# A hybrid decoder trunk on one core: low parts of the mLSTM's queries and keys, a copy of the attention keys' low half, and the sum of sink and maximum, from VectorE to GpSimd

## The chip, the core and the metric

The kernel runs on one core of a Trainium2 chip. The engines of a core are TensorE (PE: matrix products and transposes into PSUM; PEld is its weight load), VectorE (DVE), ScalarE (ACT), GpSimd (POOL) and SyncE (SP, here a DMA queue). Each has an instruction stream of its own and works through it in order; an instruction that needs another engine's result waits on a semaphore, and whatever stands behind it on its engine waits too. The metric is the device time of one execution in microseconds (us), the median over runs.

## The reference, cut to what matters

Two layers on 512 tokens of width 1024, all in float32. Each layer normalises x, multiplies by one combined matrix W_in, runs two branches and merges them through sigmoid gates, then a squared-ReLU MLP follows.

```python
q_a, k_a, v_a, q_m, k_m, v_m, o_m, if_m, gates = jnp.split(h @ w_in, splits, axis=-1)
# branch A: causal attention, window 128, 8 query heads on 2 key heads, head dimension 64,
# queries and keys normalised and partly rotated, a learned sink per head
m = jnp.maximum(jnp.max(scores, axis=-1, keepdims=True), sink)
p = jnp.exp(scores - m)
probs = p / (jnp.sum(p, axis=-1, keepdims=True) + jnp.exp(sink - m))
out = probs @ v
# branch B: mLSTM (matrix memory, 4 heads, queries and keys of 64, values of 128)
w = jnp.exp(log_d - m_t) * (q @ k.T)
num, den = w @ v + ..., jnp.sum(w, -1) + ...
h = num / jnp.maximum(jnp.abs(den), jnp.exp(-m_t))
# merge
mixed = sigmoid(g_a) * (att @ w_att_branch) + sigmoid(g_m) * (hm @ w_m_branch)
x = x + mixed @ w_out
x = x + relu(rmsnorm(x) @ w_ff1) ** 2 @ w_ff2
```

## The kernel before, in words

**Precision by splitting.** Nearly every operand of a product is split into a high part (its copy in the type fp32r, on ACT) and a low part (the float32 value less the high part, on DVE), and a product is made of three matmuls: high by high, high by low, low by high (`mm3`, L214). For a weight tile of 128x512, `chunk` (L169) issues the load on SP's queue, the copy on ACT (L195) and the subtraction on DVE (L196).

**The main stream.** A layer's projections are chains of such products, in steps of 128 rows of the weights (`group_steps`, L219). `weave` (L257) goes through the steps with a running position, each step having a width (0.25 for one output tile of a group), and calls side work when the position reaches the place that the side work was given. Attention and the mLSTM are such side work. The stretch that concerns us is L761 to L869: the projections for the mLSTM's queries and keys, gates and values are the main stream; beside them run, for each block b of 128 tokens and each key head kv (8 units a layer):

- `rope` (L569) for queries and keys, on GpSimd but for the first multiplication;
- `q_tr` (L608): four transposes into one PSUM tile, then for two tiles and two halves of the partitions ACT copies the high part (L622) and DVE forms the low part (L623);
- `k_tr` (L591): a transpose of the keys; for each key head ACT writes the high part twice, into both halves of the partitions (L600, L601), DVE forms the low part in one half (L602) and copies it into the other (L603);
- `att_scores` (L626), twice for a unit: score matmuls into PSUM; the destination is filled with a large negative number by GpSimd for block 0 (L643) or filled by ACT (L645), and DVE copies where the mask allows (L646), which also frees the PSUM tile;
- `att_softmax` (L648): DVE reduces the maximum (L653) and forms m, the negated maximum of scores and sink (L654), and es = sink + m (L656); ACT takes four exponentials with their sums (L659) and the exponential of es (L661); DVE adds, inverts and multiplies (L662 to L664);
- `att_probs` (L666): transposes, a split (L207, L208), and for b > 0 four selects on GpSimd (L678, L680);
- `att_out` (L684): the product with the values, and its evacuation by ACT (L692) and DVE (L696), then a split into the branch's input (L699, L700).

`qk_split` (L716), eight times a layer, lays out the mLSTM's queries and keys for a product with the 64 channels in both halves of the partitions. For a query head the high part (ACT, L720) is copied by GpSimd into the other half (L722), and the low tile is cleared in one half by GpSimd (L724) and holds the subtraction in the other (DVE, L725). For a key head the high part is in one half and the subtraction goes straight into the other (DVE, L728). `m_weights` (L790) reads them after attention's stretch. `gating0` to `gating3` and the gates' evacuation (L746) are further side work on DVE.

PSUM for all this side work is two tiles that take turns (`aux`, L91). Small SBUF tiles come from rings: 24 slots of 128x512 (`slot`), 18 (`temp`).

**What sets the order.** The kernel is written against a tile framework. A planner in it goes through the program when it is built, with time estimates of its own: whenever an engine is free in its plan, the instruction comes next that is ready and stands earliest in the program (those under `tc.high_priority()` ahead of others). The instruction streams that result are fixed; on the chip each engine works its stream in order. The weight splits of `chunk` are under high priority. So an instruction that changes its engine or its duration in the plan can change the order on every engine. For example, L724 stands behind L722 in the code, but in the trace two L724 run on GpSimd from 66.13 us and the first L722 at 69.66 us.

Of the kernel before, what the change touches and what calls it, by code (L numbers as in the profile page):

```python
# [13 lines left out]
ALU = mybir.AluOpType  # L14
# [21 lines left out]
def hybrid_kernel(ctx, tc, x, norm_mix, w_in, att_q_norm, att_k_norm, att_sinks, m_gate_bias,  # L36
# [3 lines left out]
    ve, sc, gp = nc.vector, nc.scalar, nc.gpsimd  # L40
# [32 lines left out]
    def slot(dt=F32, shape=(P, T)):  # L73
        return now["act"].tile(list(shape), dt, tag="a", name=nm("a"))
# [16 lines left out]
    def aux(shape=(P, T)):  # L91
        return paux.tile(list(shape), F32, tag="aux", name=nm("aux"))

    def sm(shape, tag, bufs=None):
        return small.tile(list(shape), F32, tag=tag, name=nm(tag), bufs=bufs)

    def f32(ap):
        return ap.bitcast(F32)
# [40 lines left out]
    sinks = const.tile([P, DEPTH, HQ], F32, name="sinks")  # L139
# [294 lines left out]
    def mixer(l, norm, late, order, phase):  # L434
# [113 lines left out]
        for b in range(NB):  # L548
# [5 lines left out]
                         op=ALU.mult)  # L554
# [7 lines left out]
        kTh, kTl = kT[:, 0], kT[:, 1]  # L562
# [28 lines left out]
        def k_tr(b):  # L591

            ps = aux([P, P])
            pe.transpose(ps, kvi[:, b, 0:128], ident)
            for h in range(HKV):
                r = slice(64 * h, 64 * h + 64)
                o = slice(64 - 64 * h, 128 - 64 * h)
                c = slice((b + 1) * P, (b + 2) * P)
                g = gcols[1][r, l:l + 1]
                sc.activation(kTh[r, h, c], ps[r, :], AF.Copy, scale=g)  # L600
                sc.activation(kTh[o, h, c], ps[r, :], AF.Copy, scale=g)  # L601
                ve.scalar_tensor_tensor(kTl[r, h, c], ps[r, :], g, f32(kTh[r, h, c]), op0=ALU.mult, op1=ALU.subtract)  # L602
                ve.tensor_copy(kTl[o, h, c], f32(kTl[r, h, c]))  # L603

        def q_vec(b):
            rope(q_tok[b].rearrange("p (h d) -> p h d", d=HD), b, HQ)
# [41 lines left out]
        def att_softmax(b, kv):  # L648
            sp = sps[b, kv]
            s3 = sp.rearrange("p (h k) -> p h k", h=4)  # L650
            hs = slice(4 * kv, 4 * kv + 4)
            m = sm([P, 4], "m")
            ve.tensor_reduce(m, s3, axis=AX.X, op=ALU.max)  # L653
            ve.scalar_tensor_tensor(m, m, -1.0, nsinks[:, l, hs], op0=ALU.mult, op1=ALU.min)  # L654
            es = sm([P, 4], "es")
            ve.tensor_tensor(es, sinks[:, l, hs], m, op=ALU.add)  # L656
            den = sm([P, 4], "den")
            for i in range(4):
                sc.activation(s3[:, i, :], s3[:, i, :], AF.Exp, bias=m[:, i:i + 1],  # L659
                              accum_out=den[:, i:i + 1])  # L660
            sc.activation(es, es, AF.Exp)  # L661
            ve.tensor_tensor(den, den, es, op=ALU.add)  # L662
            ve.reciprocal(den, den)
            ve.tensor_tensor(s3, s3, den.unsqueeze(2).to_broadcast([P, 4, P]), op=ALU.mult)  # L664
# [51 lines left out]
        def qk_split(m, i):  # L716
            t = qk_raw[m]
            r, o = slice(64 * i, 64 * i + 64), slice(64 - 64 * i, 128 - 64 * i)
            d = slot(F32R)
            sc.activation(d[r], t[r], AF.Copy)  # L720
            if m < 2:
                gp.tensor_copy(d[o], f32(d[r]))  # L722
                low = slot(F32R)
                gp.memset(f32(low[o]), 0.0)  # L724
                ve.tensor_tensor(low[r], t[r], f32(d[r]), op=ALU.subtract)  # L725
                m_q[2 * m + i], m_ql[2 * m + i] = d, low
            else:
                ve.tensor_tensor(d[o], t[r], f32(d[r]), op=ALU.subtract)  # L728
                m_k[2 * (m - 2) + i] = d

        def sigmoid(tiles):
# [22 lines left out]
        def ev_v(b, ps):  # L754
            if b == 0:
# [5 lines left out]
        units = [(b, kv) for b in range(NB) for kv in range(HKV)]  # L761
        side = [(0, lambda: k_vec(0)), (0, lambda: q_vec(0)), (0, lambda: k_vec(1)), (0, lambda: q_vec(1)),
                (7 - 1.25, lambda: k_tr(0)), (7 - 1.75, lambda: q_tr(0))]
        for i, (b, kv) in enumerate(units):
            at = 7 + 1.65 * i
            side += [(at, lambda b=b, kv=kv: att_scores(b, kv, 0)),
                     (at + 1.25, lambda b=b, kv=kv: att_scores(b, kv, 1)),
                     (at + 1.25, lambda b=b, kv=kv: att_softmax(b, kv)),
                     (at + 3.45, lambda b=b, kv=kv: att_probs(b, kv)),
                     (at + 3.45 + 2.2, lambda b=b, kv=kv: att_out(b, kv))]  # L770
            if kv == 0 and b + 1 < NB:
                if b + 2 < NB:
                    side += [(at + 1, lambda b=b: k_vec(b + 2)), (at + 1, lambda b=b: q_vec(b + 2))]
                side += [(at + 2 * 1.65 - 1.25, lambda b=b: k_tr(b + 1)), (at + 2 * 1.65 - 1.75, lambda b=b: q_tr(b + 1))]
        side += [(8.45 + 3.0 * i, f) for i, f in enumerate((gating0, gating1, gating2, gating3))]
        side += [(9.6 + 1.65 * n, lambda n=n: qk_split(n // 2, n % 2)) for n in range(8)]
        g0, s0 = gate_steps(0)
        g1, s1 = gate_steps(1, lambda: back(sigmoid(g0 + g1)))
# [539 lines left out]
```

## Time and profile before

| | |
|---|---|
| median of 3 runs | 1310.29 us (1309.8 to 1310.82) |
| the profiled execution | 1310.1 us, of which the span from the first to the last instruction is 1308.4 us |
| granted TensorE clock | 1.000 |
| busy in the span | PE 1290.5 us, DVE 966.4 us, ACT 781.4 us, POOL 234.6 us |

The trace has one record for each instruction: its engine, line, start and duration. In rows of the timeline the columns are start, duration, engine, line, operation, output<-input, partitions x elements and the count of instructions merged; the bracket at the end is idle time of that engine just ahead, and what ended it. A row of the waits reads: who waited for whom, us in total, how often, the longest. Rows of groups give the count, busy time and mean. The ends of matmuls are modelled, so a wait of PE can be a little longer than its idle time shows. A line of a helper (L47 and L51 for PE) stands for all callers; the tile's name tells them apart: mm is the main stream, aux the side work.

### The profile page before, as it was taken

Reading aid. Unit: us, or ns where it says so; the run is one execution under the profiler, and the core shown is the slowest. Engines: PE = TensorE matmul, PEld = TensorE weight load, DVE = VectorE, ACT = ScalarE, POOL = GpSimd, SP = SyncE. Lnnn points to the kernel's source line nnn. Section 1 sums busy time; section 2 is a strip of 40 time slices with the busy share of each in tenths; the row PEclk is TensorE's granted clock in tenths of the full one; section 3 lists DMA queues with packets and bytes.
Section 4 is the critical chain, followed back from the end, with each engine's and each line's share of the span. In section 5 each row is a group of like instructions: output and inputs, shape, how many; then the busy total and the mean of one; then the engine's idle time right before and its main releaser. Section 6 shows DMA issues by size and latency. Waiting matters only on the chain.

```text
span 1308.4 us, 19608 instructions
## 1 busy us (share of the span) xinstructions
PE 1290.5 (99%) x7126; PEld 1109.7 (85%) x7126; DVE 966.4 (74%) x1507; ACT 781.4 (60%) x1393; POOL 234.6 (18%) x331
## 2 busy tenths in 40 slices
PE   9999999999999999999999999999999999999998
PEld 7877788888899999999888777888888999999987
DVE  4688764467588897979847887645756888879786
ACT  5568765545376656667544787564544766656663
POOL 4512311100011132220115023110001111313100
PEclk9999999999999999999999999999999999999999
DMA  5422136748298989776314222367482899897743
GB/s 154 111 72 73 57 96 153 186 122 225 69 213 198 262 175 243 180 175 201 97 37 121 62 74 64 105 153 177 124 254 49 196 234 247 177 257 149 189 146 129
DMA packets 139169, 196.52 MB, mean 150 GB/s; under 512 B 10424, under 2 KB 76576, under 8 KB 139072
## 3 DMA queue, kind: packets, MB, share of 16 engines
q1 hardware_dynamic: 93040, 135.88, 34.0%
q0 software_dynamic: 37568, 44.17, 21.7%
q10 hardware_dynamic: 8464, 15.21, 3.7%
q8 instruction: 56, 0.92, 0.3%
q14 instruction: 41, 0.34, 0.1%
HBM read 193.14 MB, written 31.46 MB: 172 GB/s over the span
## 4 chain that ended last, share of the span: by engine, by line
PE 88%; DVE 7%; ACT 2%; issue 1%; DMA 1%; POOL 0%; DVEq 0%; SPq 0%; ACTq 0%; POOLq 0%
PE mm L47 75%; PE aux L47 11%; PE aux L51 2%; DVE wl L196 1%; DMA raw<-in_w_ff_dram 1%; DVE t L646 1%; DVE t L696 1%; ACT t L659 0%; DVE t L623 0%; ACT wh L195 0%; DVE a L725 0%; DVE a L876 0%; ACT wh L920 0%; DVE a L728 0%; DVE m L653 0%
## 5 line engine op out<-in xcount | busy, mean ns | idle before, releaser
L47 PE MATMUL mm<-i,wh 128*128 128x512 f32 (+1 forms) x1216 | 325.1, 354 | 0.0
L924 DVE TENSOR_TENSOR wl<-raw,wh 128x1024 fp32r<-128x1024 f32 x218 | 263.9, 1219 | 55.5 <-ACT wh L920 55.1
L920 ACT ACTIVATE wh<-raw 128x1024 fp32r<-128x1024 f32 x218 | 229.4, 1056 | 122.7 <-PE mm L47 49.9
L47 PEld LDWEIGHTS mm<-i,wh 128*128 128x128 f32 x1216 | 210.4, 190 | 26.3
L196 DVE TENSOR_TENSOR wl<-w,wh 128x512 fp32r<-128x512 f32 (+1 forms) x208 | 142.3, 685 | 118.4 <-ACT wh L195 110.7
L47 PE MATMUL mm<-i,wl 128*128 128x512 f32 (+1 forms) x608 | 214.2, 352 | 0.0
L195 ACT ACTIVATE wh<-w 128x512 fp32r<-128x512 f32 (+1 forms) x208 | 127.3, 612 | 144.3 <-PE mm L47 113.9
L47 PE MATMUL mm<-wh,uh 128*128 128x512 f32 x448 | 175.0, 391 | 0.0
L47 PE MATMUL mm<-wl,uh 128*128 128x512 f32 x448 | 174.7, 390 | 0.0
L47 PE MATMUL mm<-wh,ul 128*128 128x512 f32 x448 | 174.3, 389 | 0.0
L964 POOL DMA_DIRECT2D raw<-in_w_ff_dram x56 | 72.7, 1299 | 483.7 <-DVE wl L924 258.2
L47 PE MATMUL mm<-wh,i 128*128 128x512 f32 (+1 forms) x512 | 149.1, 368 | 0.4 <-ACT wh L195 0.4
L47 PEld LDWEIGHTS mm<-i,wl 128*128 128x128 f32 x608 | 115.1, 189 | 15.1
L47 PE MATMUL mm<-hs,wh 128*128 128x256 f32 x672 | 122.2, 283 | 0.7 <-ACT u L1155 0.7
L47 PEld LDWEIGHTS mm<-hs,wh 128*128 128x128 f32 x672 | 105.6, 192 | 2.0 <-ACT u L1155 0.9
L47 PEld LDWEIGHTS mm<-wh,i 128*128 128x128 f32 x512 | 91.6, 188 | 15.7 <-ACT wh L195 0.8
L47 PEld LDWEIGHTS mm<-wh,ul 128*128 128x128 f32 x448 | 84.1, 188 | 17.9
L47 PEld LDWEIGHTS mm<-wh,uh 128*128 128x128 f32 x448 | 84.3, 188 | 16.3
L47 PEld LDWEIGHTS mm<-wl,uh 128*128 128x128 f32 x448 | 84.3, 188 | 15.9
L47 PE MATMUL mm<-hs,wl 128*128 128x256 f32 x336 | 95.1, 283 | 0.0
L47 PE MATMUL mm<-wl,i 128*128 128x512 f32 (+1 forms) x256 | 94.0, 367 | 0.0
L978 DVE SCALAR_TENSOR_TENSOR x<-mm,ninv,x 128x512 f32<-128x512 f32 x112 | 80.0, 744 | 17.1 <-PE mm L47 17.1
(246 smaller groups left out, 2201.8 us busy)
## 6 DMA issues: line engine op xcount, KB each, us to landing
raw<-in_w_ff_dram SPq DMA_DIRECT2D x124, 512.0 KB, 5.7
w<-in_w_in_dram SPq DMA_DIRECT2D x128, 256.0 KB, 2.7
raw<-in_w_ff_dram POOLq DMA_DIRECT2D x56, 512.0 KB, 8.3
sum<-in_w_ff_dram ACTq DMA_DIRECT2D x28, 512.0 KB, 5.6
raw<-sum SPq DMA_DIRECT2D x28, 512.0 KB, 4.7
sum<-in_w_ff_dram POOLq DMA_DIRECT2D x20, 512.0 KB, 6.6
w<-in_w_out_dram SPq DMA_DIRECT2D x32, 256.0 KB, 3.5
w<-in_w_att_branch_dram SPq DMA_DIRECT2D x16, 256.0 KB, 2.6
```

Of the source, the lines that this page charges most:

```text
L47: return nc.tensor.matmul(*args, **kw)
L51: return nc.tensor.transpose(*args)
L195: last_wh[:] = sc.activation(wh[:, :off], raw[:, :off], AF.Copy), wh
L196: ve.tensor_tensor(wl[:, :off], raw[:, :off], f32(wh[:, :off]), op=ALU.subtract)
L646: ve.copy_predicated(dst, tri_i.unsqueeze(1).to_broadcast([P, 2, P]), p4[:, :, 1, :])
L696: ve.tensor_tensor(b3[64 * i:64 * i + 64], p4[:, :, i, :], l4[:, :, i, :], op=ALU.add)
L920: last_wh[:] = sc.activation(hi, r, AF.Copy), hi[:, 0, :]
L924: ve.tensor_tensor(lo, r, f32(hi), op=ALU.subtract)
L964: nc.gpsimd.dma_start(r, w1_block(k, n, c0), accum_op=ALU.add)
L978: ve.scalar_tensor_tensor(xh[:, i, :], ps[i], norm.inv[:, 0 if sign > 0 else 1, b:b + 1], xh[:, i, :], op0=ALU.mult, op1=ALU.add)
```

## The change

Four instructions in the loops above go from DVE (`ve`) to GpSimd (`gp`). Nothing else is edited; for each layer that is 8 copies, 8 small additions, 4 low parts of queries and 4 of keys.

```diff
@@ k_tr
                 ve.scalar_tensor_tensor(kTl[r, h, c], ps[r, :], g, f32(kTh[r, h, c]), op0=ALU.mult, op1=ALU.subtract)
-                ve.tensor_copy(kTl[o, h, c], f32(kTl[r, h, c]))
+                gp.tensor_copy(kTl[o, h, c], f32(kTl[r, h, c]))
@@ att_softmax
             es = sm([P, 4], "es")
-            ve.tensor_tensor(es, sinks[:, l, hs], m, op=ALU.add)
+            gp.tensor_tensor(es, sinks[:, l, hs], m, op=ALU.add)
@@ qk_split
                 gp.memset(f32(low[o]), 0.0)
-                ve.tensor_tensor(low[r], t[r], f32(d[r]), op=ALU.subtract)
+                gp.tensor_tensor(low[r], t[r], f32(d[r]), op=ALU.subtract)
                 m_q[2 * m + i], m_ql[2 * m + i] = d, low
             else:
-                ve.tensor_tensor(d[o], t[r], f32(d[r]), op=ALU.subtract)
+                gp.tensor_tensor(d[o], t[r], f32(d[r]), op=ALU.subtract)
                 m_k[2 * (m - 2) + i] = d
```

## The prediction

> **What bounds the kernel now.** I read the page first: the span, the busy shares and the chain that ended last.
>
> ```profile
> span 1308.4 us, 19608 instructions
> PE 1290.5 (99%) x7126; PEld 1109.7 (85%) x7126; DVE 966.4 (74%) x1507; ACT 781.4 (60%) x1393; POOL 234.6 (18%) x331
> PE 88%; DVE 7%; ACT 2%; issue 1%; DMA 1%; POOL 0%; DVEq 0%; SPq 0%; ACTq 0%; POOLq 0%
> ```
>
> TensorE (PE) is the bound. It is idle for 1308.4 - 1290.5 = 17.9 us in all, and no change to VectorE (DVE) work can earn more than those gaps of it that DVE ends. All edited lines run while attention is interleaved with the other projections, so next I asked for busy time in that stretch of each layer, and for what PE waited for in the first.
>
> ```profile
> core 0: us, PE busy (x) PEld busy (x) DVE busy (x) ACT busy (x) POOL busy (x), PEclk, DMA share, GB/s
> 60.00:172.00 112.00, 107.30 (x521) 83.25 (x520) 90.77 (x222) 83.12 (x219) 30.69 (x58) 1.00 0.24 69
> 708.00:820.00 112.00, 107.23 (x521) 83.25 (x520) 90.97 (x221) 82.96 (x219) 30.83 (x59) 1.00 0.25 69
> ```
>
> ```profile
> PE aux L51 <- DVE t L646: 2.2, 4, 1.4
> PE aux L47 <- DVE t L696: 0.6, 1, 0.6
> PE aux L47 <- DVE t L646: 0.5, 1, 0.5
> PE aux L51 <- DVE t L664: 0.4, 1, 0.4
> PE aux L51 <- DVE t L696: 0.3, 1, 0.3
> ```
>
> PE is idle 112 - 107.30 = 4.70 us there, and 4.77 us in the second layer, whose row is so alike that I work out one layer and double it. Of the 4.70 us, 2.2 + 0.6 + 0.5 + 0.4 + 0.3 = 4.0 us end on a DVE instruction. The whole prize is therefore at most 2 x 4.0 = 8.0 us (0.6%), whatever DVE saves.
>
> **What DVE loses.** The four edited lines, grouped, in the first layer's stretch (count | busy us, mean ns | idle before):
>
> ```profile
> L728 DVE TENSOR_TENSOR a<-a,a 64x512 fp32r<-64x512 f32 x4 | 3.4, 852 | 0.1
> L725 DVE TENSOR_TENSOR a<-a,a 64x512 fp32r<-64x512 f32 x4 | 2.9, 718 | 0.1
> L603 DVE CAST kT<-kT 64x128 fp32r<-64x128 f32 x8 | 1.8, 228 | 0.3
> L656 DVE TENSOR_TENSOR es<-sinks,m 128x4 f32<-128x4 f32 x8 | 1.6, 201 | 0.1
> ```
>
> That is 3.4 + 2.9 + 1.8 + 1.6 = 9.7 us of DVE's 90.77. It counts only where it stands ahead of a PE gap. The gaps that have a moved line ahead of them:
>
> ```profile
> 79.11 0.30 PE L51 MATMUL aux<-ident,kvi 128*128 128x128 f32 x1 [1.42 <-DVE t L646]
> 115.40 0.71 PE L47 MATMUL aux<-kT,t 128*128 128x256 f32 x4 [0.65 <-DVE t L696]
> 137.42 0.63 PE L51 MATMUL aux<-ident,t 128*128 128x128 f32 x4 [0.17 <-DVE t L646]
> ```
>
> **The first gap (1.42 us).** DVE and ScalarE (ACT) in the microseconds ahead of it:
>
> ```profile
> 70.65 0.82 DVE L725 TENSOR_TENSOR a<-a,a 64x512 fp32r<-64x512 f32 x1
> 72.81 0.16 DVE L654 SCALAR_TENSOR_TENSOR m<-m,nsinks 128x4 f32<-128x4 f32 x1
> 73.01 0.48 DVE L623 SCALAR_TENSOR_TENSOR t<-aux,gc,t 64x256 fp32r<-64x256 f32 x1
> 73.60 1.40 DVE L725 TENSOR_TENSOR a<-a,a 64x512 fp32r<-64x512 f32 x2
> 75.02 0.69 DVE L196 TENSOR_TENSOR wl<-w,wh 128x512 fp32r<-128x512 f32 x1
> 76.76 0.49 DVE L623 SCALAR_TENSOR_TENSOR t<-aux,gc,t 64x256 fp32r<-64x256 f32 x1
> 78.52 0.45 DVE L646 COPY_PREDICATED t<-tri_l,aux 128x256 f32<-128x256 int32 x1
> ```
>
> ```profile
> 71.57 0.47 ACT L622 ACTIVATE t<-aux,gc 64x256 fp32r<-64x256 f32 x1 [0.67 <-PE aux L51]
> 73.01 0.40 ACT L659 ACTIVATE t<-t,m 128x128 f32<-128x128 f32 x1 [0.31 <-DVE m L654]
> 75.09 0.19 ACT L661 ACTIVATE es<-es 128x4 f32<-128x4 f32 x1
> 75.30 0.47 ACT L622 ACTIVATE t<-aux,gc 64x256 fp32r<-64x256 f32 x1
> ```
>
> All four L725 stand here, 2.9 us, ahead of the L646 that sets PE free; so the gap can close entirely: 1.42 us is the upper end. The lower end comes from ACT. The second L622 at 75.30 stands behind the exponentials, which began at 73.01 after a wait of 0.31 us for the negated maximum m (L654). Without the L725 in front of L654 that wait goes, and little else of ACT's row moves: 0.31 us. What lies between is the order. Each pair of L622 (ACT) and L623 (DVE) takes turns on one PSUM tile; the first L623 could run as soon as L622 has ended (72.04) instead of at 73.01. The order of each engine is set at build time by a planner with estimates of its own, and it will plan anew. I take the middle, (1.42 + 0.31) / 2 = 0.87, call it 0.9 us.
>
> **The second gap (0.65 us).** Two L728 run for 2.05 us ahead of it, then a weight split and the softmax's division:
>
> ```profile
> 110.71 2.05 DVE L728 TENSOR_TENSOR a<-a,a 64x512 fp32r<-64x512 f32 x2
> 112.79 0.69 DVE L196 TENSOR_TENSOR wl<-w,wh 128x512 fp32r<-128x512 f32 x1
> 112.83 0.19 ACT L661 ACTIVATE es<-es 128x4 f32<-128x4 f32 x1
> 113.40 0.15 DVE L662 TENSOR_TENSOR den<-den,es 128x4 f32<-128x4 f32 x1
> ```
>
> L662 needs L661's result (113.02) and starts at 113.40, so at the least 0.2 us and at the most the gap's 0.65 can be won; the 2.05 us themselves cannot, since ACT's exponentials end no earlier. I take 0.35, nearer to ACT's end.
>
> **The third gap (0.17 us)** has an L603 in its chain, of 0.228 us by its group: all of 0.17 goes, from 0 if the copy comes back late. The other gaps (0.5 us <- L646, 0.3 us <- L696, 0.4 us <- L664 and the rest of L646's) end chains in which no moved instruction stands: zero.
>
> Sum for one layer: 0.9 + 0.35 + 0.17 = 1.4 us; for two, 2.8 to 2.9 us.
>
> **What GpSimd (POOL) gains.** The trace shows no two-input operation on 64x512 there; the nearest rows (min/median/max ns):
>
> ```profile
> L550 POOL TENSOR_TENSOR t<-a x8: 1037/1040/1227, 33.6 to 684.7; 128x512 f32<-128x512 f32 x8
> L722 POOL CAST a<-a x8: 608/612/975, 69.7 to 721.2; 64x512 fp32r<-64x512 f32 x8
> L579 POOL TENSOR_TENSOR rq<-kvi,st x8: 218/444/665, 53.0 to 710.8; 128x16 f32<-128x16 f32 x8
> ```
>
> A low part costs between 0.61 (one input, same shape) and 1.04 us (two inputs, same row length); I take 1.04, since the kind of operation and the row length agree. The sum es costs 0.22 us by L579's shortest, the copy of the keys' half between DVE's 0.23 and 0.61; I take 0.3. One layer: 8 x 1.04 + 8 x 0.22 + 8 x 0.3 = 12.5 us, so POOL goes from 30.69 to 43 us of 112. That is hidden as long as nothing in its queue is late. Where it stands idle:
>
> ```profile
> 73.59 0.56 POOL L643 MEMSET t<- 128x256 f32 x2
> 108.25 0.64 POOL L678 TENSOR_SCALAR_AFFINE_SELECT t<-t 128x512 fp32r<-128x512 f32 x1 [34.09 <-ACT t L207]
> 108.98 1.16 POOL L680 TENSOR_SCALAR_AFFINE_SELECT t<-t 128x512 fp32r<-128x512 f32 x1
> ```
>
> From 74.15 to 108.25 it waits. The four low parts of the queries (4.2 us) fit there; their reader, the mLSTM's product, comes after the stretch. The new waits: ACT's L661 waits for POOL, and behind it on ACT are L622 and the weight splits that feed PE. In the first softmax m is there at 72.97 and L661 runs at 75.09: 2.1 us of room, which one low part ahead of es (1.04 + 0.22) does not use up and two (2.3) just do.
>
> At 108 us the keys' four low parts meet the selects. The select at 108.98 took 1.16 us and the two L728 at 110.71 averaged 1.03 us, against 0.69 us for the subtraction L196 behind them, and 0.64 us for the select ahead: both engines lose when they work from SBUF at once. The Trainium skill (GPSIMD Engine Reference, section 1, Specifications) says that GpSimd shares its SBUF interfaces with VectorE and contends with its two-input instructions; this row agrees. The same page (section 4.1, Engine selection) advises against this very move, putting two-input elementwise work on GpSimd at about twice VectorE's time; by it the low parts would cost 2 x 0.69 = 1.38 us (an estimate) and POOL's addition 15 us, while L550 (1.04 us) against that L196 (0.69 us), both 128x512, gives 1.5 times. Neither takes POOL to its limit.
>
> **Rivals.**
> Contention and ACT take the relief back. If every low part on POOL lengthens a DVE instruction beside it by 1.03 - 0.69 = 0.34 us, the four before the first gap give back 1.4 us, all of its 0.9; what is left is the third gap and part of the second, 0.2 to 0.3 us a layer: 1309.8, no change. For it: the L728 beside the selects. Against it: POOL has 34 idle microseconds, most of them beside PSUM work of DVE.
>
> A wait on POOL takes the place of the ones removed: slower. Place: the queue at 70 to 78 us. Decided by how many low parts are planned ahead of es (or of the memsets at 73.59, which the L646 at 78.52 needs). With all four ahead, es is ready 4 x 1.04 + 0.22 = 4.4 us after m, 2.3 us later than L661 wants it; ACT stands, L622 and a weight split behind it, and PE's first gap grows by 2.3 us. Two layers: +4.6 us, 1314.9; with three ahead +1.2 us a layer, 1312.8. From two on it begins to cost. For it: POOL serves in order, and its memsets at 73.59 already run behind four L722. Against it: es stands before the low parts in the code, and the memsets end 4.4 us before that L646 starts.
>
> The planner turns all the relief into order: the L622/L623 pairs move forward and the gaps behind L646 and L696 close, 2 to 4 us a layer, 1302 to 1306. For it: 9.7 us of DVE gone where DVE is 81% busy. Against it: ACT is 74% busy in the same stretch and stands in most of these chains.
>
> **How the numbers follow.** The profiled execution took 1310.1 us (span 1308.4 and 1.7 around it), the median of the runs 1310.29, 0.2 above it. Less 2.9 that is 1307.4 us on the median. What a measurement can tell from no change is about 0.2%, 2.6 us: below 1307.7 is faster, above 1312.9 slower. The forecast's own range follows from the ends of its terms: 0.31 + 0.2 + 0 = 0.5 us a layer at the least, 1.42 + 0.65 + 0.17 = 2.2 us at the most, so 1305.8 to 1309.3. Chances: the forecast 0.40 (0.26 of it faster), the planner's full relief 0.15, all given back 0.18 (0.16 within 0.2%, 0.01 to each side), POOL late 0.27 (0.26 slower). Faster 0.26 + 0.15 + 0.01 = 0.42; same 0.14 + 0.16 + 0.01 = 0.31; slower 0.26 + 0.01 = 0.27. The range, 1303.5 to 1313.5, holds the forecast, the middle case, most of the full relief, and the late POOL up to three low parts ahead; left out are the ends of both, some 0.2.
>
> **What would show it.** Right: the edited lines stand on POOL; DVE's busy time in the two stretches falls by 8 to 10 us each and POOL's rises by 10 to 14; PE's first gap is 0.3 to 0.8 us, the second 0.2 to 0.4, the third gone; L661 shows no wait for POOL. Wrong: ACT idle before L661 ended by POOL, or PE waiting for L678, L680 or the keys' copy (POOL late); PE's gaps unchanged while DVE has fallen (ACT holds them); low parts of 0.6 or of 1.4 us on POOL; or new gaps behind lines that wait for nobody now, which would be the plan's order and no step above.

## The result, and the profile after

The changed kernel takes 1317.8 us in the median of 6 executions (1315.59 to 1318.12), the kernel before 1310.15 beside it. The ratio is 1.0055, 95% interval 1.0044 to 1.0066: slower by 7.6 us. The forecast was 1307.4 us with a range up to 1313.5; it was wrong in sign, and the result lies outside its range.

The page of the profiled execution (1318.05 us), its span and busy shares:

```profile
span 1316.3 us, 19607 instructions
PE 1295.0 (98%) x7126; PEld 1113.9 (85%) x7126; DVE 955.0 (73%) x1459; ACT 781.5 (59%) x1393; POOL 263.4 (20%) x379
```

DVE lost 11.4 us and POOL gained 28.8. PE is busy 4.5 us longer with the same 7126 matmuls, so some matmuls ran slower, and the clock has to be looked at as well as the gaps. Busy time by engine in the two stretches of attention, with the granted clock as the first figure behind the engines:

```profile
60.00:172.00 112.00, 105.67 (x502) 82.83 (x501) 82.09 (x186) 79.19 (x207) 44.36 (x80) 0.97 0.24 66
708.00:820.00 112.00, 105.41 (x502) 82.77 (x502) 82.36 (x186) 76.22 (x200) 47.40 (x88) 0.97 0.24 68
```

In the same 112 us 502 matmuls are recorded on PE instead of 521, and the mean clock is 0.97, not 1.00. The moved lines in the groups of the first stretch (count | busy us, mean ns):

```profile
L725 POOL TENSOR_TENSOR a<-a,a 64x512 fp32r<-64x512 f32 x4 | 5.6, 1402 | 0.3
L728 POOL TENSOR_TENSOR a<-a,a 64x512 fp32r<-64x512 f32 x4 | 5.1, 1283 | 5.3 <-ACT a L720 5.1
L603 POOL CAST kT<-kT 64x128 fp32r<-64x128 f32 x8 | 2.6, 330 | 21.1 <-DVE kT L602 21.0
L656 POOL TENSOR_TENSOR es<-sinks,m 128x4 f32<-128x4 f32 x8 | 2.1, 268 | 11.2 <-DVE m L654 10.8
```

They cost POOL 15.4 us in this layer, not the 12.5 of the sum. PE's idle time, by gap:

```profile
82.07 0.45 PE L51 MATMUL aux<-ident,kvi 128*128 128x128 f32 x1 [3.12 <-DVE t L646]
...
118.53 0.71 PE L47 MATMUL aux<-kT,t 128*128 128x256 f32 x4 [0.74 <-DVE t L696]
121.31 0.66 PE L51 MATMUL aux<-ident,a 128*128 128x128 f32 x4 [0.68 <-DVE t L646]
```

The first gap, 1.42 us before, is 3.12; the second is 0.74 instead of 0.65; a new one of 0.68 stands behind it. What the prediction calls the third gap, 0.17 us, is 0.20 us here (at 141.70 us). What leads to the first one is in the chain of waits (start, duration, what; the copies, the fill and the low parts of POOL, and their reader):

```profile
75.26 1.08 POOL a L722
...
76.87 1.29 POOL a L725
...
79.33 1.75 POOL a L725
...
81.13 0.33 POOL t L643
...
81.48 0.45 DVE t L646
```

POOL is hardly idle from 70.92 us on. The last two low parts run ahead of the fill L643, and DVE's L646, which frees the PSUM tile for PE, waits for that fill. Then the clock, in slices of 2 us behind the gap (PE's busy time with the number of matmuls, then the clock):

```profile
80.00:82.00 2.00, 0.00 (x0) 0.82 0.44 122
82.00:84.00 2.00, 1.93 (x8) 0.50 0.03 9
84.00:86.00 2.00, 2.00 (x6) 0.50 0.25 45
86.00:88.00 2.00, 2.00 (x8) 0.50 0.22 86
```

For 6 us behind the gap the clock is at half. One and the same kind of matmul shows it in its duration, before and after:

```profile
80.62 0.39 PE L47 MATMUL mm<-i,wl 128*128 128x512 f32 x1
```

```profile
84.87 0.63 PE L47 MATMUL mm<-i,wl 128*128 128x512 f32 x1
```

From 88 us on the clock is back at 0.98 and more. The second layer shows the same at 734 to 740 us.

Where the 7.9 us of span came in can be read from two evacuations that follow PE: the mLSTM's last keys (L714) and the gate sums (L510). The last two columns of times are the first and the last start, in the first layer. Before:

```profile
L714 DVE TENSOR_TENSOR a<-mm,t x2: 680/680/681, 68.5 to 69.7; 128x512 f32<-128x512 f32 x2
L510 DVE COPY bl<-aux x1: 192/192/192, 84.8 to 84.8; 128x32 f32<-128x32 f32 x1
L836 DVE TENSOR_TENSOR a<-a,mm x8: 679/684/689, 178.1 to 195.5; 128x512 f32<-128x512 f32 x8
```

After:

```profile
L714 DVE TENSOR_TENSOR a<-mm,t x2: 679/682/684, 69.7 to 71.0; 128x512 f32<-128x512 f32 x2
L510 DVE COPY bl<-aux x1: 191/191/191, 89.5 to 89.5; 128x32 f32<-128x32 f32 x1
L836 DVE TENSOR_TENSOR a<-a,mm x7: 681/686/690, 182.8 to 198.9; 128x512 f32<-128x512 f32 x7
```

(The last view ends at 200 us, so one L836 is missing in it.) From L714 to L510 it was 84.8 - 69.7 = 15.1 us and is 89.5 - 71.0 = 18.5: +3.4 us, the gap and the slow clock together; the second layer has the same 15.1 and 18.5. From L510 to the first L836 behind the stretch it is 93.3 us in both, so nothing is won later either. The remaining 1.3 us of the first layer arise ahead of L714: 0.7 ahead of the first projection's evacuation, which starts at 32.8 us before, at 33.5 here, and between 32.8 and 34.6 in the other kernels without an order to it, and 0.6 up to L714, which goes with the copy L603 (below).

### The profile page after: what moved, and what is told of

It reads as the page before. It is cut to its first block, busy times and chain, and to the rows that moved or that the text cites. A ratio compares the mean times of both kernels' runs of the same rounds, so it can differ in the third digit from the quotient of the medians.

```text
span 1316.3 us, 19607 instructions
## 1 busy us (share of the span) xinstructions
PE 1295.0 (98%) x7126; PEld 1113.9 (85%) x7126; DVE 955.0 (73%) x1459; ACT 781.5 (59%) x1393; POOL 263.4 (20%) x379
## 4 chain that ended last, share of the span: by engine, by line
PE 85%; DVE 5%; ACT 3%; POOL 2%; DMA 2%; issue 2%; DVEq 0%; SPq 0%; ACTq 0%; POOLq 0%
PE mm L47 73%; PE aux L47 10%; PE aux L51 2%; DVE wl L196 1%; DMA w<-in_w_in_dram 1%; ACT wh L195 1%; ACT t L659 1%; DMA raw<-in_w_ff_dram 1%; POOL a L725 0%; DVE t L646 0%; DVE t L696 0%; DVE a L876 0%; DVE t L664 0%; POOL rp L576 0%; DVE u L700 0%
## 5 line engine op out<-in xcount | busy, mean ns | idle before, releaser
L47 PE MATMUL mm<-i,wh 128*128 128x512 f32 (+1 forms) x1216 | 329.5, 357 | 0.0
L196 DVE TENSOR_TENSOR wl<-w,wh 128x512 fp32r<-128x512 f32 (+1 forms) x208 | 142.4, 685 | 132.6 <-ACT wh L195 126.7
```

Of the source, the lines that this page charges most:

```text
L47: return nc.tensor.matmul(*args, **kw)
L196: ve.tensor_tensor(wl[:, :off], raw[:, :off], f32(wh[:, :off]), op=ALU.subtract)
```

## The experiments

Theory: POOL's queue is the loss. The low parts run ahead of block 0's fills, es and the copies stand in the same queue, and behind the longer gap the clock falls. Rivals: the other three edits; DVE lengthened by POOL's work beside it (contention); the order that the planner chose anew. The table gives each kernel's median, its ratio to the kernel before, timed beside it on the same chip (medians of 1309.99 to 1310.33 there), and the first gap by layer; where the plan splits that gap in two, both.

| kernel | us | ratio | first gap, us |
|---|---|---|---|
| the change | 1317.8 | 1.0055 [1.0044, 1.0066] | 3.12, 3.11 |
| q_low: only the queries' low parts | 1312.8 | 1.0023 [1.0014, 1.0032] | 2.34, 2.34 |
| rest: the other three edits | 1312.33 | 1.0018 [1.001, 1.0027] | 1.68, 1.69 |
| early: the change, fills emitted first | 1311.83 | 1.0018 [1.0009, 1.0026] | 2.42, 2.42 |
| before_early: before, fills emitted first | 1309.44 | 0.9993 [0.9985, 1.0002] | 0.71 and 0.64, 0.71 and 0.66 |
| q_x1: q_low and one more clear | 1314.01 | 1.0028 [1.0017, 1.0038] | 2.78, 2.78 |
| q_s1: q_low, one low part twice | 1316.66 | 1.0049 [1.0037, 1.0062] | 3.67, 3.67 |
| q_early: q_low, fills emitted first | 1313.06 | 1.0028 [1.0017, 1.0039] | 2.55, 2.56 |
| copy: only the copy L603 | 1309.27 | 0.9994 [0.9985, 1.0003] | 1.41, 1.42 |
| q_behind: q_low, low parts queued behind the fills | 1311.1 | 1.0008 [0.9999, 1.0017] | 1.65, 1.66 |
| after_behind: the change, queued so | 1313.01 | 1.0021 [1.0011, 1.003] | 1.65, 1.66 |
| es_k: only the sum and the keys' low parts | 1313.14 | 1.0025 [1.0016, 1.0034] | 1.68, 1.69 |
| copy_early: copy, fills emitted first | 1309.46 | 0.9993 [0.9985, 1.0002] | 0.71 and 0.63, 0.70 and 0.75 |
| q_none: the queries' low parts left out | 1308.59 | 0.9991 [0.9982, 1.0] | 1.03, 1.05 |
| es: only the sum | 1310.22 | 1.0001 [0.9992, 1.001] | 1.67, 1.69 |

### The parts: q_low, rest

q_low makes one of the edits, rest the other three.

```diff
-                ve.tensor_tensor(low[r], t[r], f32(d[r]), op=ALU.subtract)
+                gp.tensor_tensor(low[r], t[r], f32(d[r]), op=ALU.subtract)
```

> Only the queries' low parts (L725) on GpSimd. Theory 'fills behind low parts' (the four L725 of over 1.2 us each stand ahead of the fills L643 in GpSimd's queue, so L646 and with it PE wait, and the long gap lowers PE's clock): the first gap is 2.5 to 3.5 us in each layer, the clock is below 1.00 just behind it, 1315 to 1318 us. Rival 'many small losses' (contention, es and the key copy on GpSimd, a new order on PE): the first gap stays at or below 1.5 us, clock 1.000, 1308 to 1312 us.

> All of the change but the queries' low parts, which stay on VectorE. Theory 'fills behind low parts': the first gap is 1.5 us or less, clock 1.000, 1308 to 1312 us. Rival 'many small losses': 1314 us or more, with the loss spread over other gaps.

q_low came out at +2.8 us with TensorE's instructions in the very order of before. Its gap, and behind it what DVE's L646 waited for:

```profile
79.94 0.30 PE L51 MATMUL aux<-ident,kvi 128*128 128x128 f32 x1 [2.34 <-DVE t L646]
```

```profile
79.35 0.44 DVE L646 COPY_PREDICATED t<-tri_l,aux 128x256 f32<-128x256 int32 x1 [1.02 <-POOL t L643]
```

That is the rival of the prediction in its place, though smaller than the theory had it: 2.34 us, not 2.5 to 3.5, and the clock at 1.00 in the profiled execution. But rest lost 2.3 us without it, a little more than the theory allowed, and the two together, 5.1 us, are less than the change's 7.6. The traces agree: the first gap grows by 0.92 us in q_low and 0.26 in rest, and by 1.70 in the change. The edits act on one another.

### The fills ahead of the low parts, by emission: early, before_early, q_early

The fills of block 0 for both key heads are written at the first score step, so that they are planned ahead of the low parts (the fill's old place is left empty).

```diff
-            if hp == 0:
-                sps[b, kv] = temp()
+            if hp == 0 and (b, kv) not in sps:
+                sps.update({(b, n): temp() for n in ([0, 1] if b == 0 else [kv])})
...
-                gp.memset(dst, NEG)
+                [gp.memset(sps[0, n], NEG) for n in range(2) if kv + hp == 0]
```

> The whole change, and block 0's fills of both key heads are put in front of everything else of the first unit, so that they stand ahead of the low parts in GpSimd's queue. Theory 'fills behind low parts': no wait of L646 for GpSimd, the first gap 1.5 us or less, clock 1.000, 1306 to 1311 us. Rival 'many small losses': the other gaps stay and it is 1314 us or more.

> The kernel before with the same early fills: the control for the plan's new order that this edit makes by itself. Both theories: nothing waited for the fills there, so 1308 to 1312 us; what it differs from 1310.2 by is what a new order alone does.

> The queries' low parts on GpSimd and block 0's fills ahead of them; PE's order differs by a few rows from that of before_early (1309.4 us), which it is to be held against. Theory 'fills behind low parts': L646 doesn't wait for GpSimd and the gaps stay within 0.5 us of those of before_early, 1308.5 to 1310.5 us. Rival 'contention': the low parts cost by themselves, DVE's instructions beside them are longer and PE's gaps grow, 1311.5 us or more.

The change with this repair gets back most of the 7.6 us: 6.0 by the medians, 4.8 by the ratios. It still missed the theory's numbers (1311 us at the most, a gap of 1.5 us at the most): its gap is 2.42 us, and ends on a key's low half (L602) and no longer on L646. q_early missed the theory's number: no L646 waits for POOL any more, and still the gap is 2.55 us, where the kernel before with the same edit has two of 0.71 and 0.64. In q_early the plan is another one (TensorE's order too), the gap now ends on a key's low half, and the copy in that chain stretches beside a low part on POOL from 0.22 to 1.05 us:

```profile
77.89 1.05 DVE L603 CAST kT<-kT 64x128 fp32r<-64x128 f32 x1
...
80.59 0.22 DVE L603 CAST kT<-kT 64x128 fp32r<-64x128 f32 x1
```

So the wait for the fill could not be all, and emission order is too blunt a tool: it makes a new plan.

### The wait alone, in steps: q_x1, q_s1

More work in POOL's queue ahead of the fill, nothing else: on the other engines the order is that of q_low. For the last query head, q_x1 clears the low half once more (the diff), q_s1 forms the low part twice (0 clears and 2 subtractions there).

```diff
-                gp.tensor_tensor(low[r], t[r], f32(d[r]), op=ALU.subtract)
+                [gp.memset(f32(low[o]), 0.0) for _ in range(1 if m + i == 2 else 0)], [gp.tensor_tensor(low[r], t[r], f32(d[r]), op=ALU.subtract) for _ in range(1 if m + i == 2 else 1)]
```

> The queries' low parts on GpSimd as in q_low, with the last head's low tile cleared once more (0.5 us more in GpSimd's queue ahead of the fills); every other engine's order is that of q_low. The first gap is then 2.3 + 0.55 = 2.9 us. If PE's clock falls behind a gap only from some length between 2.4 and 3.1 us on, it may or may not fall here: with the clock at 1.00, 1313.9 us (1312.8 + 2 x 0.55); with the clock fallen in both layers another 2 x 2 us, 1317 to 1318.5 us. Rival, the clock in the changed kernel fell for another reason (other engines' load): clock 1.00 here and at every longer gap.

> As q_low, with the last head's low part computed twice on GpSimd (1.33 us more ahead of the fills), every other engine's order that of q_low. The first gap is 3.7 us in each layer. Theory 'a long gap lowers PE's clock': clock 0.5 for some 6 us behind it in both layers, 1312.8 + 2 x (1.33 + 2) = 1319 to 1320 us. Rival, the clock fell in the changed kernel for another reason: clock 1.00, 1312.8 + 2 x 1.33 = 1315.5 us.

Over two layers the gap grew by 0.9 and 2.7 us against q_low. The loss, each kernel against the kernel before beside it, grew from 2.8 us to 3.7 and 6.3, so by 0.9 and 3.6; the intervals are over 1 us wide on either side, and these numbers alone show no excess over the gap. The clock did fall, in both layers of both profiled executions, where the profiled execution of q_low, with the same orders, had 1.00: so lengthening the gap is enough to lower it. But the fall is cheaper than the theory had it. q_x1 was to take 1317 us or more with the clock fallen, q_s1 1319, and both stayed below. From L714 to L510, 15.1 us before, q_low takes 16.1 and 16.0 us, which is the gap's growth of 0.92; q_x1 takes 18.3 and 17.0, q_s1 17.9 and 18.9, which is 0.5 to 1.8 us a layer more than the gap's growth. In q_s1's second layer (PE busy, clock):

```profile
732.00:734.00 2.00, 1.28 (x5) 0.50 0.00 0
734.00:736.00 2.00, 2.00 (x9) 0.50 0.00 0
736.00:738.00 2.00, 2.00 (x8) 0.50 0.47 131
```

### POOL's order alone: q_behind, after_behind

The low part is written later and told to follow the last fill in POOL's queue (its line in the trace is then L704, the helper). TensorE, DVE and ACT keep the orders of q_low and of the change, instruction by instruction.

```diff
+        def after_fill(f, *a, **k):
+            with tc.issue_after(fills[-1].ins):
+                f(*a, **k)
...
-                gp.tensor_tensor(low[r], t[r], f32(d[r]), op=ALU.subtract)
+                lows.append(lambda: after_fill(gp.tensor_tensor, low[r], t[r], f32(d[r]), op=ALU.subtract))
...
-        side += [(9.6 + 1.65 * n, lambda n=n: qk_split(n // 2, n % 2)) for n in range(8)]
+        side += [(9.6 + 1.65 * n, lambda n=n: qk_split(n // 2, n % 2)) for n in range(8)] + [(11.6 + 1.65 * n, lambda n=n: lows[n]()) for n in range(4)]
```

> Only the queries' four low parts (L725) on GpSimd, and its queue told to take them behind the last of block 0's fills (L643); TensorE, VectorE and ScalarE have the orders of the kernel that only moves them (gap 2.34 us, 1312.8), in which L646 waited 1.02 us for that fill. Theory A (GpSimd's queue alone): the 1.02 us go and the gap is the old 1.42 us less what VectorE gained, 0.5 to 1.4 us; 1308.5 to 1310.5. Theory B (the plan's new order on ScalarE, exponentials ahead of the first L622, and VectorE stretched beside GpSimd): L646 waits for no fill, but L664 runs at 1.0 us or more beside the low parts and the gap stays at 1.8 to 2.4 us; 1311.5 to 1313.

> The whole change with the same arrangement of GpSimd's queue (low parts behind the last fill); the other engines' orders are those of the change, whose gap was 3.12 us and whose time 1317.8. Theory A: the fill's wait (1.02 us) and the sum es and the low parts ahead of it go: gap 1.4 us or less, clock 1.00, 1309.5 to 1312. Theory B: the gap falls to 2.1 to 2.6 us, the clock falls to half in at most one of the layers: 1311.5 to 1315.

Nothing but the order of POOL's queue differs between after_behind and the change, and the time falls from 1317.8 to 1313.01, and the ratio by 0.0034: 4.5 to 4.8 of the 7.6 us were that order, give or take some 2 us by the intervals. The gap fell from 3.12 to 1.65 us, and the clock stays at 1.00:

```profile
80.73 0.30 PE L51 MATMUL aux<-ident,kvi 128*128 128x128 f32 x1 [1.65 <-DVE t L646]
```

```profile
80.00:82.00 2.00, 1.27 (x8) 1.00 0.45 131
82.00:84.00 2.00, 1.44 (x6) 1.00 0.19 31
```

q_behind's gap is also 1.65 us, in both kernels between the two theories' numbers (up to 1.4, and from 1.8 on): DVE is relieved of 2.9 us of work ahead of it and the gap is still longer than the 1.42 of before. DVE in q_behind ahead of the gap, beside low parts on POOL from 76.98 us on:

```profile
76.04 0.91 DVE L664 TENSOR_TENSOR t<-t,den 128x512 f32<-128x512 f32 x1
76.99 0.49 DVE L623 SCALAR_TENSOR_TENSOR t<-aux,gc,t 64x256 fp32r<-64x256 f32 x1
77.51 1.31 DVE L196 TENSOR_TENSOR wl<-w,wh 128x512 fp32r<-128x512 f32 x1
```

### Contention or the plan's order: q_none

The low parts of the queries are left out altogether; POOL clears their half of the tile instead, so this kernel leaves a part of the mLSTM's queries away. The orders of TensorE, DVE and ACT are those of q_behind and q_low.

```diff
-                ve.tensor_tensor(low[r], t[r], f32(d[r]), op=ALU.subtract)
+                gp.memset(f32(low[r]), 0.0)
```

> The four low parts of the queries (L725) left out, on every engine: their half of the tile is cleared by GpSimd instead, so the mLSTM's queries lose their low part. TensorE, VectorE and ScalarE keep the orders of the kernels with L725 on GpSimd (gap 2.34 us with the queue as planned, 1.69 us with the fills ahead). If contention of two-input work on GpSimd eats the relief, L664 and L196 run at 0.69 us here and the gap is 0.7 to 1.1 us: 1308 to 1309.5. If the order on ScalarE eats it (exponentials ahead of the first L622), the gap stays at 1.4 us or more though nothing contends: 1310 to 1311.5.

The time (1308.59) and the gap (1.03) lie where the expectation has them for contention.

```profile
80.38 0.30 PE L51 MATMUL aux<-ident,kvi 128*128 128x128 f32 x1 [1.03 <-DVE t L646]
```

```profile
77.10 0.91 DVE L664 TENSOR_TENSOR t<-t,den 128x512 f32<-128x512 f32 x1
78.03 0.49 DVE L623 SCALAR_TENSOR_TENSOR t<-aux,gc,t 64x256 fp32r<-64x256 f32 x1
78.55 0.69 DVE L196 TENSOR_TENSOR wl<-w,wh 128x512 fp32r<-128x512 f32 x1
```

The one DVE instruction of this chain that differs is the weight split L196, 0.69 instead of 1.31 us: 0.62 us, and the gap is 1.65 - 1.03 = 0.62 us shorter. That part of the loss is contention, shown. L664 still takes 0.91 us here, not the 0.69 that was expected: it runs beside the copy L722 on POOL (76.84 to 77.45 us). That is 0.22 us more than before. The rest I put down to ACT: even with the four low parts gone from every engine the gap shrinks only by 1.42 - 1.03 = 0.39 us, since the chain of L622 and L623 starts later. Because m is ready sooner, the plan puts the exponentials ahead of the first L622, in the change too:

```profile
72.97 0.40 ACT L659 ACTIVATE t<-t,m 128x128 f32<-128x128 f32 x1 [0.80 <-DVE m L654]
...
75.27 0.47 ACT L622 ACTIVATE t<-aux,gc 64x256 fp32r<-64x256 f32 x1
```

Before, L622 started at 71.57 and the exponentials at 73.01. A kernel that keeps the old order on ACT with the low parts gone was not run, so that the order is the cause of the small relief is read from these rows and not shown by a run of its own.

### The other three edits: copy, copy_early, es, es_k

> Only the copy of the keys' low half (L603) on GpSimd. Theory 'copy behind the rope': the first block's copies stand behind the rotations (L576 to L581) in GpSimd's queue and PE waits for them with its first score product, 0.4 to 1.5 us in each layer, 1310.5 to 1313 us. Rival: the copies are in time as the prediction had it, 1309 to 1310.3 us.

> Only the copy (L603) on GpSimd, with block 0's fills emitted first. Each alone saved about 0.5 to 1 us a layer in attention's stretch. If they add up: 1307.5 to 1309. If they earn the same gap twice: 1309 to 1310.5.

> Only the sum es (L656) and the keys' low parts (L728) on GpSimd. With the copy as well it was 1312.3, and the copy alone 1309.3 (nothing). If the terms add up, 1312 to 1313.5, with L728 on GpSimd beside the selects and a longer wait at TensorE behind L696 or L678/L680. Rival: the copy was what lost there, through the 1.45 us of TensorE behind L603 and the clock's fall after it; then 1309.5 to 1311 and no clock below 0.9.

> Only the sum es (L656) on GpSimd. If the sum pushes the fourth copy L722 to where it stands beside L725 on VectorE and lengthens it (1.40 to 1.73 us for two, as with es and the keys' low parts moved), the first gap is 1.6 to 1.7 us and the time 1310.5 to 1311.3. If es does nothing by itself, the gap is 1.42 us or less and the time within 0.3 us of before, and the keys' low parts carry all of that kernel's loss.

Each makes only the edits that it names, with the lines of the change (copy_early adds the emission edit from above).

copy lost nothing, against the theory's 1310.5 to 1313. Its copy does stand behind the rotation of later blocks in POOL's queue, and PE waits for it in the second layer (no such wait shows in the first):

```profile
713.48 0.45 POOL L581 TENSOR_TENSOR a<-rp,rq 128x128 f32<-128x128 f32 x1
714.00 0.84 POOL L603 CAST kT<-kT 64x128 fp32r<-64x128 f32 x1
```

```profile
714.89 0.55 PE L47 MATMUL aux<-kT,t 128*128 128x128 f32 x3 [1.25 <-POOL kT L603]
```

From the layer's last key projection (L465) to L714 it takes 23.3 and 23.7 us, 22.6 and 22.5 before. In the six kernels with this copy on POOL it is 23.1 to 23.7 us, in the ten without 22.3 to 23.0. It wins about as much in attention's stretch, 107.4 us from L714 to L836 in both layers and 108.4 and 108.5 before. copy_early, which was to add up the two small gains, is no faster than either: none of the three can be told from the kernel before.

es leaves the time alone (1310.22, under the 1310.5 that was expected), though it lengthens the first gap to 1.67 us, as expected. The sum of 0.20 us pushes the fourth copy L722 to a place beside L725 on DVE, two of which then take 1.73 us instead of 1.40:

```profile
73.53 0.20 POOL L656 TENSOR_TENSOR es<-sinks,m 128x4 f32<-128x4 f32 x1
73.80 0.61 POOL L722 CAST a<-a 64x512 fp32r<-64x512 f32 x1
```

```profile
73.93 1.73 DVE L725 TENSOR_TENSOR a<-a,a 64x512 fp32r<-64x512 f32 x2
```

es_k lost 2.9 us, as much as its terms added up to, with the clock at 1.00 in the profiled execution. What it adds to es is the keys' low parts, so they, not the copy, carry the loss of rest. A keys' low part on POOL stands beside the division L664, and behind that a gap appears that before had not (DVE, then PE):

```profile
115.48 1.71 DVE L664 TENSOR_TENSOR t<-t,den 128x512 f32<-128x512 f32 x1
```

```profile
118.47 0.63 PE L51 MATMUL aux<-ident,a 128*128 128x128 f32 x4 [0.77 <-DVE t L646]
```

## Why the prediction was wrong

**The step that failed** is the cover given to the queries' low parts: "The four low parts of the queries (4.2 us) fit there", in POOL's idle time from 74.15 us on, and its ground against the late POOL: "the memsets end 4.4 us before that L646 starts". The idle time lies behind the fills; the low parts were planned ahead of them. The rival had the place right ("or of the memsets at 73.59, which the L646 at 78.52 needs") and named four low parts as its case. The path that it priced was another one, the sum es late for L661, and that did not happen: es runs at 73.64 us behind one low part, and L661 at 75.05, with no wait for POOL. The 4.4 us of margin were used up, and more: the fill went from 73.59 to 81.13 us, with 1.3 us of a later start, four low parts of 1.40 on the mean, the sum es and a copy L722 of 1.08 ahead of it. The ladder of kernels with the same order on the other three engines (from q_none on) shows what each costs in the first gap: 1.42 us before, 1.03 with the relief alone (q_none), 1.65 with contention (q_behind), 2.34 with the fill behind the low parts (q_low); es and the other edits in the same queue bring it to 3.12, and after_behind, where only the queue differs, back to 1.65.

**The first gap's gain of 0.9 us** was the middle of two ends. The lower end, 0.31, is near the 0.39 us that came when the low parts were on no engine (q_none), but by luck. It stood for exponentials that start 0.31 us sooner; reckoned from the last L714, they start 3.3 us behind it before and 2.0 in q_none and in the change, 1.3 us sooner. The prediction expected the first L622 to move forward as well; the plan moved the exponentials forward and L622 back.

**The price of a low part**, 1.04 us from L550, was too small: 1.28 us at the shortest and 1.30 where DVE stood idle (73.92 us), against 0.69 on DVE, 1.86 times, and up to 1.75 beside DVE. Here the Trainium skill was nearer than the row that I preferred: the GPSIMD Engine Reference (section 4.1, Engine selection) gives about twice for two-input work. The estimate of 1.38 us that the prediction made from it stands beside 1.28 measured; the group's mean with contention is 1.40.

**Contention** was priced at 0.34 us for an instruction, and held unlikely because most of POOL's idle time lay beside PSUM work of DVE. That reading was wrong: of DVE's 30 us of work between 74 and 108 us before, under half (13.5 us) reads a PSUM tile. Contention is also larger (L664 0.69 to 1.59 and 1.71, L196 0.69 to 1.31), and it struck in the chain. By q_behind and q_none it costs 0.62 us of gap a layer.

**The second gap's 0.35 us** did not come: 0.74 against 0.65. With es alone it is 0.56, with the keys' low parts as well (es_k) 0.73, so they take the gain back. In the change two instructions of DVE ahead of the L696 that ends this gap run longer beside POOL's work than before (0.69 and 0.15):

```profile
116.11 0.90 DVE L196 TENSOR_TENSOR wl<-w,wh 128x512 fp32r<-128x512 f32 x1 [0.99 <-ACT wh L195]
116.94 0.58 DVE L662 TENSOR_TENSOR den<-den,es 128x4 f32<-128x4 f32 x1
```

The division L664, at 118.42 us, stands behind that L696 and ahead of the new gap of 0.68. How much of the second gap is ACT's, whose exponentials the prediction named, was not tried by itself.

**The third gap's 0.17 us** did not close: 0.20 in the change, and 0.22 with the copy alone moved, so L603 did not set it. What the copy did cost stands elsewhere, and the prediction had it only as a bound ("from 0 if the copy comes back late"): PE reaches L714 0.6 to 0.7 us later in each layer.

**The clock** was in no step. A gap was counted at its own length; the change pays more, because TensorE is at half speed behind it. The kernel early shows the price within one kernel: its twelve executions run from 1309.16 us at a mean clock of 0.999 to 1315.04 at 0.995. The change ran at 0.995 to 0.998. The profiled executions of early and q_early also show the price between their two layers, where the gaps are the same and the clock falls in the second alone: from L714 to L510 early takes 14.8 and 16.2 us, q_early 15.0 and 17.7. There a fall cost 1.4 and 2.7 us.

**The sum after the fact:** from L714 to L510 the change takes 3.4 us more in each layer, of which 1.70 are the gap's growth; the other 1.7 I put down to the clock, and the price in early and q_early agrees. At half speed for 6 us PE does 3 us' less work; part of that falls into waits that the kernel before has there, such as the 0.48 us ahead of its score product at 81.95 us, which are gone. So of the 7.9 us of span 3.4 are the gap, 3.4 the clock and 1.3 the copy; the 0.7 us ahead of the first projection come on top, and some 0.9 are made up elsewhere. The order of POOL's queue carries the gap's last 1.47 us and the clock together. What after_behind still loses, 2.8 us, is about what es_k loses.

## What to carry to other kernels

Before moving work to an engine that looks idle, look at where its idle time stands in its queue: work that becomes ready ahead of a short instruction that others wait for delays it by its whole length, however much idle time follows. Price the move at what both engines lose while they run side by side, and where the bound is TensorE, look at the clock behind a gap that grows: here a fall behind gaps of 2.4 us and more cost 0.5 to 2.7 us on top of the gap. When it has gone wrong, reordering that one queue with all other orders held fixed tells in one kernel how much of the loss is the queue.

## What the runs showed of the hardware that was not expected

**The clock falls behind gaps of less than 3 us.** With a first gap of up to 1.42 us (before) or of 1.65 to 1.69 us (q_behind, after_behind, es, es_k) the clock stays at 1.00 behind it in the profiled executions (one other execution of q_behind has a mean of 0.997, two of es_k 0.998); with 2.34 us (q_low) it was 1.00 in the profiled one, while the mean clock over the span of the others was 0.997 to 0.999; with 2.42 and 2.55 us (early, q_early) it fell in one layer of two, with 2.78 us and more in both. The Trainium skill (TensorE: Matmul & The Clock Gate, Part 1: The HAM clock gate) names an idle window of about 3.4 us that runs freely, and a fall after a whole idle one. That executions of one kernel differ agrees with a window that is not tied to the program; that 2.42 us were enough does not agree with a whole idle window of 3.4 us. In rest the clock fell to 0.56 and 0.58 for 4 us in the second layer though no gap there was above 1.69 us, and after_behind had the same gaps without a fall; why is open.

**Contention reaches one-input work.** The Trainium skill (GPSIMD Engine Reference, section 1, Specifications) names VectorE's instructions with two SBUF inputs, and those in a 2-port mode. L664 and L196, with two inputs, agree (up to 1.71 and 1.31 us against 0.69). The one-input copy L603 on DVE, 0.22 us, took 1.05 beside a low part on POOL in q_early; in which mode it runs, no row shows.
